# A graph-attention layer: turn-and-score in one matmul, division for two blocks at once, blocks of 125 targets in place of 121

## The chip, the cores and the metric

The kernel runs on one core of one Trainium2 chip. The metric is the device time of one execution in microseconds (us). Each time quoted is the median of several runs; a ratio is the mean time of one kernel's fast runs over the mean of the other's fast runs of the same rounds, so it is not quite the ratio of the medians. The engines are called PE (TensorE), DVE (VectorE), ACT (ScalarE), POOL (GpSimd) and SP (SyncE, which here only issues DMA). A one-hot is a matrix that has a 1 where an edge's node number matches the row and 0 elsewhere; PSUM is the memory that this kernel's matmuls write to; the span is the time from the first to the last instruction of the profiled run, and the quoted time is some 2 us more (317.16 against 314.9 before).

## The reference

There are 4096 nodes with 64 features, 50000 edges and 4 heads of 64 outputs. Cut to what matters:

```python
x_proj[h] = x @ weight[h]
score[h, e] = sum(x_proj[h, src] * att_src[h]) + sum(x_proj[h, dst] * att_dst[h])
score = where(score > 0, score, 0.2 * score)
output[h, dst] += exp(score[h, e]) * x_proj[h, src]        # over all edges
output[h, dst] /= (sum of exp(score[h]) over edges to dst) + 1e-8
```

## The kernel before

The first 120 us sort the edges on DVE into bins: one bin holds the edges whose target is in one block of `BD = 121` nodes and whose source is in one of 16 groups of 256 nodes. A bin has room for 128 edges, so a block is 16 tiles of 128 edges. Then 34 blocks are worked off. For each block:

```python
# load: the block's targets and sources, broadcast to all partitions (1 MB), DMA on SP
# onehot (DVE): oh[:,0] target one-hot, oh[:,1] and oh[:,2] source one-hots
# gather (PE, per tile t): three matmuls into xps[:, t, 0:72]
T.matmul(out=o, lhsT=oh[:, 1, e], rhs=xa[:, 2 * t, :], ...)            # 64 features + 8 scores
T.matmul(out=o, lhsT=oh[:, 2, e], rhs=xa[:, 2 * t + 1, :], ...)
T.matmul(out=o[:, Din:XC], lhsT=oh[:, 0, e], rhs=adb[:, b, :], ...)    # 8 target scores
# ACT: ex = exp(scores); xs = copy of the features
# turn (PE): 16 transposes of oh[:, 0], then two ACT copies to Sb
# weigh (DVE): wv = max(ex[:,0], ex[:,1]); val = xs * wv   (128 x 4096, bf16)
# scatter (PE): 16 denominators (4 columns), 32 accumulations of Sb[:, t, 0:BD]
# Finish: ACT copies the sums to aT (a second small copy adds 1e-8);
#         PE projects them with the weights; DVE: inv = 1/aT, res = pf * inv; DMA out
def run(self):
    self.onehot(0); self.gather(0); self.turn(0); self.onehot(1)
    for b in range(ND):
        self.load(b + 3)
        self.weigh(b, 2 if b == ND - 1 else 1)
        self.gather(b + 1)
        self.turn(b + 1)
        self.onehot(b + 2)
        if b:
            self.sink.give(b - 1)
        self.scatter(b)
    self.sink.give(ND - 1)
```

Each engine takes its own instructions in this program order, as PE's chain in the prediction shows: turn at 238.42, projection 239.33, denominators 239.82, sums 240.22, the next gather 241.97. `gather(b + 1)` and `turn(b + 1)` stand ahead of `scatter(b)`, so no matmul that feeds the next `val` waits behind one that needs this `val`.

## Time and profile before

| | before |
|---|---|
| time, median of the first 3 runs | 317.16 us |
| span of the profiled run | 314.9 us |
| to the start of the first `val` | 138.0 us |
| first to last `val` (33 intervals) | 162.6 us |
| from the start of the last `val` to the end | 14.3 us |
| busy in the stretch 147 to 200 us: PE, DVE, ACT | 100%, 96%, 73% |

The useful ruler is the start of `val`, DVE's big multiplication, once a block. The three parts add up to the span. The main views are in the prediction. Two more groups, by shape, are needed to see what the change takes out. The columns are line, engine, operation, tiles, shapes and count, then busy time and mean ns of one, then the idle time before it.

```profile
L437 ACT COPY Sb<-sp 128x1024 bf16<-128x1024 bf16 x68 | 66.3, 1039 | 0.0
L506 DVE TENSOR_TENSOR res<-pf,inv 121x256 f32<-121x256 f32 x34 | 14.4, 425 | 3.4 <-PE pf L501 0.4
```

The first is ACT's largest part, the copies of the turned one-hots. The second is the division, with 34 instructions.

### The profile page before, as it was taken

To read this page: it belongs to the slowest core of one execution; us is meant where nothing else is said; L and a number is where in the kernel's file an instruction comes from. 1 tells how busy PE (TensorE), PEld (TensorE's weight loads), DVE (VectorE), ACT (ScalarE), POOL (GpSimd) and SP (SyncE) were. 2 spreads that over 40 slices of the span, in tenths; PEclk is the share of its full clock that TensorE was granted. 3 is DMA by queue.
4 is the path that set the end of the run, shared out by engine and by line. 5 is a ranking of instruction groups with operands and counts; after the bars stand their busy time and mean duration, and the time that the engine had idled before them with its cause. 6 is when DMAs were issued, how large, how long until landed. Compare 5 with 4: busy or idle time off the path is not lost. (4 is left out here: it accounts for less than half of the span.)

```text
span 314.9 us, 9697 instructions
## 1 busy us (share of the span) xinstructions
PE 207.2 (66%) x4122; PEld 202.2 (64%) x4122; DVE 275.9 (88%) x552; ACT 172.9 (55%) x324; POOL 18.6 (6%) x40
## 2 busy tenths in 40 slices
PE   0049999000000000099999999999999999999970
PEld 0027999000000000099999999999999999999970
DVE  8999999993999995479999999999999999999960
ACT  3984000000999600067777768677686767768640
POOL 6800000002000005000000000000000000000000
PEclk9999555555555555579999999999999999999996
DMA  7200000002000002991865857667575766667110
GB/s 206 46 1 0 2 0 0 1 0 67 1 0 0 0 28 51 300 395 32 284 234 224 290 191 271 216 237 251 204 276 191 258 228 253 232 227 272 56 38 21
DMA packets 13551, 43.97 MB, mean 140 GB/s; under 512 B 3308, under 2 KB 8492, under 8 KB 9148
## 3 DMA queue, kind: packets, MB, share of 16 engines
q1 hardware_dynamic: 11332, 41.92, 37.7%
q10 hardware_dynamic: 1464, 0.70, 0.8%
q0 software_dynamic: 704, 0.66, 0.8%
q8 instruction: 34, 0.56, 0.8%
q14 instruction: 17, 0.14, 0.2%
HBM read 38.22 MB, written 5.05 MB: 137 GB/s over the span
## 5 line engine op out<-in xcount | busy, mean ns | idle before, releaser
L449 DVE TENSOR_TENSOR val<-xs,wv 128x4096 bf16<-128x4096 bf16 (+1 forms) x35 | 78.0, 2231 | 4.1 <-ACT xs L423 0.7
L437 ACT COPY Sb<-sp 128x1024 bf16<-128x1024 bf16 x68 | 66.3, 1039 | 0.0
L413 PE MATMUL xps<-xa,oh 128*128 128x72 bf16 x544 | 54.1, 194 | 14.5 <-DVE oh L401 14.5
L463 PE MATMUL acc<-Sb,val 128*128 128x121 bf16 x1088 | 63.6, 217 | 0.0
L413 PEld LDWEIGHTS <-oh 128*128 128x128 bf16 x544 | 50.4, 98 | 13.9 <-DVE oh L400 13.9
L463 PEld LDWEIGHTS <-val 128*128 128x128 bf16 x1088 | 58.5, 98 | 0.1
L415 PE MATMUL xps<-xa,oh 128*128 128x72 bf16 x544 | 53.7, 195 | 0.1
L417 PE MATMUL xps<-adb,oh 128*128 128x8 bf16 x544 | 52.8, 169 | 0.0
L415 PEld LDWEIGHTS <-oh 128*128 128x128 bf16 x544 | 49.4, 96 | 1.2 <-DVE oh L401 1.1
L417 PEld LDWEIGHTS <-oh 128*128 128x128 bf16 x544 | 50.1, 97 | 0.0
L400 DVE TENSOR_SCALAR oh<-bc,pF 128x4096 bf16<-128x4096 bf16 x34 | 43.5, 1281 | 4.6 <-DMA bc<-gat_bins 4.6
L420 ACT ACTIVATE ex<-xps 128x256 bf16<-128x256 f32 x34 | 13.4, 395 | 58.3 <-PE xps L417 58.3
L188 DVE TENSOR_TENSOR sA<-sB 128x256 f32<-128x256 f32 (+2 forms) x108 | 39.6, 408 | 1.8
L250 ACT ACTIVATE junk<-kr,nb 128x512 f32<-128x512 f32 x34 | 24.5, 722 | 25.6 <-DVE kr L301 24.5
L188 DVE TENSOR_TENSOR sB<-sA 128x256 f32<-128x256 f32 (+2 forms) x100 | 36.7, 408 | 1.7
L261 PE MATMUL cnt_ps<-sgn,sel 128*128 128x17 f32 (+1 forms) x6 | 1.7, 390 | 53.1 <-ACT sgn L253 53.1
L436 PE MATMUL sp<-identb,oh 128*128 128x128 bf16 x544 | 36.5, 221 | 0.0
L261 PEld LDWEIGHTS cnt_ps<-sgn,sel 128*128 128x128 f32 x6 | 1.4, 318 | 53.2 <-issue 53.2
L423 ACT CAST xs<-xps 128x1024 bf16<-128x1024 f32 x34 | 34.1, 1003 | 0.0
L436 PEld LDWEIGHTS <-oh 128*128 128x128 bf16 x544 | 31.4, 99 | 0.0
L401 DVE TENSOR_SCALAR oh<-bc,pF 128x2048 bf16<-128x2048 bf16 x34 | 25.4, 747 | 0.0
L345 PEld LDWEIGHTS at_ps<-uv,xT 64*128 64x128 f32 x132 | 25.1, 297 | 0.4 <-issue 0.4
(116 smaller groups left out, 255.7 us busy)
## 6 DMA issues: line engine op xcount, KB each, us to landing
bc<-gat_bins SPq DMA_DIRECT2D x34, 1024.0 KB
out_dram<-res SPq DMA_DIRECT2D x33, 121.0 KB
gat_sorted<-sA SPq DMA_DIRECT2D x2, 256.0 KB
eS<-in_edge_index_dram SPq DMA_DIRECT2D x1, 390.0 KB
eD<-in_edge_index_dram ACTq DMA_DIRECT2D x1, 390.0 KB
gat_bins<-tb ACTq DMA_DIRECT2D x9, 32.0 KB
out_dram<-res SPq DMA_DIRECT2D x1, 103.0 KB
win<-gat_sorted,wi POOLq DMA_INDIRECT x5, 2.6
```

What stands on the lines that cost most here:

```text
L188: V.tensor_tensor(out=av(d[:], o, [2 * h, n], [1, h]), in0=av(s[:], 0, [2 * h, n], [1, h]), in1=av(s[:], h, [2 * h, n], [1, h]), op=op)
L345: T.matmul(out=ps[:, b, :], lhsT=xT[:, b * step:b * step + P], rhs=uv[:, k, :], start=(b == 0), stop=True, skip_group_check=True)
L400: V.tensor_scalar(out=oh[:, 0:2, :], in0=bc[:], scalar1=pF[:, 0:1], scalar2=None, op0=OP.is_equal)
L401: V.tensor_scalar(out=oh[:, 2, :], in0=bc[:, 1, :], scalar1=pF[:, 1:2], scalar2=None, op0=OP.is_equal)
L413: T.matmul(out=o, lhsT=oh[:, 1, e], rhs=xa[:, 2 * t, :], start=(t % 4 == 0), stop=False, skip_group_check=True)
L415: T.matmul(out=o, lhsT=oh[:, 2, e], rhs=xa[:, 2 * t + 1, :], start=False, stop=False, skip_group_check=True)
L417: T.matmul(out=o[:, Din:XC], lhsT=oh[:, 0, e], rhs=adb[:, b, :], start=False, stop=True, skip_group_check=True)
L423: S.copy(out=xs[:], in_=xps[:, :, 0:Din])
L436: T.transpose(out=sp[:, i, :], in_=oh[:, 0, t * W2:(t + 1) * W2], identity=identb[:])
L437: S.copy(out=Sb[:, q * NT // 2:(q + 1) * NT // 2, :], in_=sp[:])
L449: V.tensor_tensor(out=av(val[:], h * Dout, [Dout, n], [C, NT], [1, Din]), in0=av(xs[:], 0, [0, n], [2, NT * Din // 2], [1, 2]), in1=av(wv[ ...
L463: T.matmul(out=acc[:, k * BD:(k + 1) * BD], lhsT=val[:, t, k * P:(k + 1) * P], rhs=Sb[:, t, 0:BD], start=False, stop=(t == NT - 1), skip_g ...
```

## The change

Its intent: one matmul with an identity beside the score columns does the turn and the target scores at once; epsilon enters as three bf16 terms through one-row matmuls, so that one copy of the sums suffices; reciprocal and division are done for two blocks at once; blocks of 125 targets make 33 blocks of 34; the first load is split over two queues. In place of one PSUM tile for all 16 gathers (128 numbers each a partition) there are two buffers of 6 (256 numbers each), so the gather is cut into three parts (6, 6 and 4 tiles), and these are put between the sums. The core of the diff, with cuts marked:

```diff
-BD = 121
+BD = 125
 ...
+    for i in range(3):                       # epsilon as three bf16 terms
+        V.tensor_copy(out=eps[:, i, :], in_=e0[:])
+        if i < 2:
+            V.tensor_copy(out=e1[:], in_=eps[:, i, :])
+            V.tensor_tensor(out=e0[:], in0=e0[:], in1=e1[:], op=OP.subtract)
 ...
-                T.matmul(out=o[:, Din:XC], lhsT=oh[:, 0, e], rhs=adb[:, b, :], start=False, stop=True,
+                T.matmul(out=ps[:, i, 0:S0], lhsT=oh[:, 0, e], rhs=adb[:, b, :], start=False, stop=True,
 ...
+            S.copy(out=xs[:, t0:t0 + n, 0:P + XC], in_=ps[:, 0:n, 0:P + XC])
 ...
-                self.gather(b + 1)
-                self.turn(b + 1)
+                self.gather(b + 1, 0)
                 self.onehot(b + 2)
                 if b:
-                    self.sink.give(b - 1)
-                self.scatter(b)
-            self.sink.give(ND - 1)
+                    self.sink.project(b - 1)
+                    if b % 2 == 0:
+                        self.sink.give(b - 2, 2)
+                self.sums(b, -1)
+                self.gather(b + 1, 1)
+                self.sums(b, 0)
+                self.gather(b + 1, 2)
+                self.sums(b, 1)
```

`sums(b, 0)` is the first matmul that needs `val` of block b; `sums(b, -1)` needs only wv.

More of the change, by code (lines that the diff above doesn't have):

```diff
@@ L110 @@
     pm8 = bits("pm8", 0, 7)
-    eps = cst.tile([P, 1], F32)
-    V.memset(eps[:], 1e-8)
+    e0 = cst.tile([1, H], F32)
+    e1 = cst.tile([1, H], F32)
+    eps = cst.tile([1, 3, H], BF16)
+    one = cst.tile([1, P], BF16)
+    nil = cst.tile([1, 3, H], BF16)
+    V.memset(e0[:], 1e-8)
+    V.memset(one[:], 1.0)
+    V.memset(nil[:], 0.0)
+    for i in range(3):
[3 more added lines that the diff above has]
+            V.tensor_tensor(out=e0[:], in0=e0[:], in1=e1[:], op=OP.subtract)
     goff = cst.tile([P, 1], F32)
@@ L150 @@
     xa = cst.tile([P, NB, XC], BF16)
-    adb = cst.tile([P, ND, 2 * H], BF16)
+    AB = P + 2 * H
+    adb = cst.tile([P, ND, AB], BF16)
     Wbd = cst.tile([P, 2, P], F32)
@@ L333, in tables @@
             S.copy(out=uv[:, :, 2 * i:2 * i + 2], in_=av(ps2[:], 0, [2, 2], [1, 2]))
-        S.copy(out=xa[:, :, 0:Din], in_=xf[:])
+        S.copy(out=xa[:, :, 2 * H:XC], in_=xf[:])
         xT = pr.tile([Din, ND * BD + P - BD], F32)
@@ L341, in tables @@
             S.copy(out=xT[:, 4 * q * P:4 * (q + 1) * P], in_=ps[:])
-        for k, (n, step, to) in enumerate(((NB, P, xa[:, :, Din:XC]), (ND, BD, adb[:]))):
+        for k, (n, step, to) in enumerate(((NB, P, xa[:, :, 0:2 * H]), (ND, BD, adb[:, :, P:AB]))):
             ps = pp1.tile([P, n, H], F32, name=f"at_ps{k}")
@@ L348, in tables @@
             S.mul(out=to[:, :, H:2 * H], in_=ps[:], mul=ALPHA)
+        S.copy(out=adb[:, :, 0:P], in_=av(identb[:], 0, [0, ND], [1, P]))
     NT = NR
@@ L374, in unpack @@
                               in_=self.tb[:, i, k, :])
+    CH = ((0, 6), (6, 6), (12, 4))
+    S0 = P + 2 * H
+    XW = 256
     class Blocks:
@@ L382, in __init__, with load, onehot @@
             self.bp = pool(name="blk", bufs=2)
-            self.psx = pool(name="ps_x", bufs=1, space=PSUM)
-            self.pss = pool(name="ps_s", bufs=2, space=PSUM)
+            self.psx = pool(name="ps_x", bufs=2, space=PSUM)
             self.psa = pool(name="ps_a", bufs=1, space=PSUM)
             self.sink = sink
-            self.bc, self.oh, self.xps, self.ex, self.xs, self.wv, self.Sb, self.val = ({} for _ in range(8))
-        def load(self, b):
+            self.bc, self.oh, self.ex, self.xs, self.wv, self.val = ({} for _ in range(6))
+        def load(self, b, engs=(nc.sync,)):
             if b < ND:
                 t = self.bcp.tile([P, 2, NT * W2], BF16, name="bc")
-                nc.sync.dma_start(out=t[:], in_=dataclasses.replace(bin_dram[b], ap=[[0, P], [NT * W2, 2],
-                                                                                    [1, NT * W2]]))
+                n = NT * W2 // len(engs)
+                for i, eng in enumerate(engs):
+                    eng.dma_start(out=t[:, :, i * n:(i + 1) * n],
+                                  in_=dataclasses.replace(bin_dram[b, 0, i * NT // len(engs)],
+                                                          ap=[[0, P], [NT * W2, 2], [1, n]]))
                 self.bc[b] = t
-        def onehot(self, b):
+        def onehot(self, b, parts=1):
             if b < ND:
@@ L399, in onehot, with gather @@
                 oh = self.bp.tile([P, 3, NT * W2], BF16, name="oh")
-                V.tensor_scalar(out=oh[:, 0:2, :], in0=bc[:], scalar1=pF[:, 0:1], scalar2=None, op0=OP.is_equal)
-                V.tensor_scalar(out=oh[:, 2, :], in0=bc[:, 1, :], scalar1=pF[:, 1:2], scalar2=None, op0=OP.is_equal)
+                n = NT * W2 // parts
+                for i in range(0, NT * W2, n):
+                    V.tensor_scalar(out=oh[:, 0:2, i:i + n], in0=bc[:, :, i:i + n], scalar1=pF[:, 0:1], scalar2=None,
+                                    op0=OP.is_equal)
+                    V.tensor_scalar(out=oh[:, 2, i:i + n], in0=bc[:, 1, i:i + n], scalar1=pF[:, 1:2], scalar2=None,
+                                    op0=OP.is_equal)
                 self.oh[b] = oh
-        def gather(self, b):
+        def gather(self, b, c):
             if b >= ND:
@@ L408, in gather @@
             oh = self.oh[b]
-            xps = self.psx.tile([P, NT, P], F32, name="xps")
-            for t in range(NT):
-                o = xps[:, t, 0:XC]
+            if c == 0:
+                self.ex[b] = self.bp.tile([P, 2, H, NT, 2], BF16, name="ex")
+                self.xs[b] = self.bp.tile([P, NT, XW], BF16, name="xs")
+            ex, xs = self.ex[b], self.xs[b]
+            t0, n = CH[c]
+            ps = self.psx.tile([P, CH[0][1], XW], F32, name="ps")
+            for i in range(n):
+                t = t0 + i
@@ L412, in gather @@
                 e = slice(t * W2, (t + 1) * W2)
-                T.matmul(out=o, lhsT=oh[:, 1, e], rhs=xa[:, 2 * t, :], start=(t % 4 == 0), stop=False,
+                T.matmul(out=ps[:, i, P:P + XC], lhsT=oh[:, 1, e], rhs=xa[:, 2 * t, :], start=(i % 2 == 0), stop=False,
                          skip_group_check=True)
-                T.matmul(out=o, lhsT=oh[:, 2, e], rhs=xa[:, 2 * t + 1, :], start=False, stop=False,
+                T.matmul(out=ps[:, i, P:P + XC], lhsT=oh[:, 2, e], rhs=xa[:, 2 * t + 1, :], start=False, stop=False,
@@ L416, in gather @@
                          skip_group_check=True)
-                T.matmul(out=o[:, Din:XC], lhsT=oh[:, 0, e], rhs=adb[:, b, :], start=False, stop=True,
+                T.matmul(out=ps[:, i, 0:S0], lhsT=oh[:, 0, e], rhs=adb[:, b, :], start=False, stop=True,
                          skip_group_check=True)
-            ex = self.bp.tile([P, 2, H, NT, 2], BF16, name="ex")
-            S.activation(out=av(ex[:], 0, [2, NT], [2 * NT, 2 * H], [1, 2]),
-                         in_=av(xps[:], Din, [P, NT], [1, 2 * H], [0, 2]), func=ACTF.Exp)
@@ L422, in gather @@
-            xs = self.bp.tile([P, NT, Din], BF16, name="xs")
-            S.copy(out=xs[:], in_=xps[:, :, 0:Din])
-            self.ex[b], self.xs[b] = ex, xs
-        def turn(self, b):
-            if b >= ND:
-                return
-            oh = self.oh.pop(b)
-            Sb = self.bp.tile([P, NT, W2], BF16, name="Sb")
-            for q in range(2):
-                sp = self.pss.tile([P, NT // 2, W2], BF16, name="sp")
-                for i in range(NT // 2):
-                    t = q * NT // 2 + i
-                    T.transpose(out=sp[:, i, :], in_=oh[:, 0, t * W2:(t + 1) * W2], identity=identb[:])
-                S.copy(out=Sb[:, q * NT // 2:(q + 1) * NT // 2, :], in_=sp[:])
-            self.Sb[b] = Sb
+            S.activation(out=av(ex[:], 2 * t0, [2, n], [2 * NT, 2 * H], [1, 2]),
+                         in_=av(ps[:], P, [XW, n], [1, 2 * H], [0, 2]), func=ACTF.Exp)
@@ L440, in weigh @@
+            S.copy(out=xs[:, t0:t0 + n, 0:P + XC], in_=ps[:, 0:n, 0:P + XC])
+            if c == len(CH) - 1:
+                self.oh.pop(b)
         def weigh(self, b, parts=1):
-            xs, ex = self.xs.pop(b), self.ex.pop(b)
+            xs, ex = self.xs[b], self.ex.pop(b)
             wv = self.bp.tile([P, H, NT, 2], BF16, name="wv")
@@ L449, in weigh @@
                 V.tensor_tensor(out=av(val[:], h * Dout, [Dout, n], [C, NT], [1, Din]),
-                                in0=av(xs[:], 0, [0, n], [2, NT * Din // 2], [1, 2]),
+                                in0=av(xs[:], S0, [0, n], [XW, NT], [1, Din]),
                                 in1=av(wv[:], h * 2 * NT, [2, n * NT], [0, Din // 2], [1, 2]), op=OP.mult)
             self.val[b] = val
-        def scatter(self, b):
-            val, wv, Sb = self.val.pop(b), self.wv.pop(b), self.Sb.pop(b)
-            acc = self.psa.tile([P, AW], F32, name="acc")
-            for t in range(NT):
-                T.matmul(out=acc[:, 2 * BD:AW], lhsT=Sb[:, t, :], rhs=av(wv[:], 2 * t, [2 * NT, H]), start=(t == 0),
-                         stop=(t == NT - 1), skip_group_check=True)
-            for k in range(2):
-                for t in range(NT):
-                    T.matmul(out=acc[:, k * BD:(k + 1) * BD], lhsT=val[:, t, k * P:(k + 1) * P], rhs=Sb[:, t, 0:BD],
-                             start=False, stop=(t == NT - 1), skip_group_check=True)
-            self.sink.take(b, acc[:])
@@ L467, in run, with sums @@
-        def run(self):
-            self.onehot(0)
-            self.gather(0)
-            self.turn(0)
+        def sums(self, b, k):
+            xs = self.xs[b]
+            if k < 0:
+                self.acc = self.psa.tile([P, AW], F32, name="acc")
+                wv = self.wv.pop(b)
+                for i in range(3):
+                    T.matmul(out=self.acc[:, 2 * BD:AW], lhsT=one[:], rhs=self.sink.first[:, i, :], start=(i == 0),
+                             stop=False, skip_group_check=True)
+                for t in range(NT):
+                    T.matmul(out=self.acc[:, 2 * BD:AW], lhsT=xs[:, t, 0:P],
+                             rhs=av(wv[:], 2 * t, [2 * NT, H]), start=False, stop=(t == NT - 1), skip_group_check=True)
+                return
+            val = self.val[b]
+            for t in range(NT):
+                T.matmul(out=self.acc[:, k * BD:(k + 1) * BD], lhsT=val[:, t, k * P:(k + 1) * P],
+                         rhs=xs[:, t, 0:BD], start=False, stop=(t == NT - 1), skip_group_check=True)
+            if k == 1:
+                self.val.pop(b), self.xs.pop(b)
+                self.sink.take(b, self.acc[:])
@@ L471, in run @@
+        def run(self, parts=1):
+            self.onehot(0, parts)
+            for c in range(len(CH)):
+                self.gather(0, c)
             self.onehot(1)
@@ L483 @@
+                self.gather(b + 1, 1)
+                self.sums(b, 0)
+                self.gather(b + 1, 2)
+                self.sums(b, 1)
+            self.sink.project(ND - 1)
+            n = 2 - ND % 2
+            self.sink.give(ND - n, n)
     class Finish:
         def __init__(self, ctx):
+            self.first = eps
             self.fp = ctx.enter_context(tc.tile_pool(name="fin", bufs=2))
             self.psf = ctx.enter_context(tc.tile_pool(name="ps_f", bufs=1, space=PSUM))
-            self.aT = {}
@@ L491, in take @@
         def take(self, b, acc):
-            aT = self.fp.tile([P, AW], F32, name="aT")
-            S.copy(out=aT[:, 0:2 * BD], in_=acc[:, 0:2 * BD])
-            S.activation(out=aT[:, 2 * BD:AW], in_=acc[:, 2 * BD:AW], func=ACTF.Identity, bias=eps[:, 0:1])
-            self.aT[b] = aT
-        def give(self, b):
-            aT = self.aT.pop(b)
-            pf = self.psf.tile([P, C], F32, name="pf")
-            for k in range(2):
-                T.matmul(out=pf[0:BD, k * P:(k + 1) * P], lhsT=aT[:, k * BD:(k + 1) * BD], rhs=Wbd[:, k, :],
-                         start=(k == 0), stop=True, skip_group_check=True)
-            inv = self.fp.tile([P, H], F32, name="inv")
-            V.reciprocal(out=inv[:], in_=aT[:, 2 * BD:AW])
-            res = self.fp.tile([P, H, Dout], F32, name="res")
-            V.tensor_tensor(out=res[0:BD], in0=av(pf[0:BD], 0, [Dout, H], [1, Dout]),
-                            in1=av(inv[0:BD], 0, [1, H], [0, Dout]), op=OP.mult)
-            n = min(BD, N - b * BD)
-            nc.sync.dma_start(out=out[b * BD:b * BD + n, :], in_=res[0:n].rearrange("p h o -> p (h o)"))
+            if b % 2 == 0:
+                self.aT = self.fp.tile([P, 2, AW], F32, name="aT")
+                self.pf = self.psf.tile([P, 2, C], F32, name="pf")
@@ new lines, in take, with project, give @@
+            S.copy(out=self.aT[:, b % 2, :], in_=acc)
+        def project(self, b):
+            for k in range(2):
+                T.matmul(out=self.pf[0:BD, b % 2, k * P:(k + 1) * P], lhsT=self.aT[:, b % 2, k * BD:(k + 1) * BD],
+                         rhs=Wbd[:, k, :], start=(b % 2 == 0 and k == 0), stop=True, skip_group_check=True)
+        def give(self, b, n):
+            inv = self.fp.tile([P, 2, H], F32, name="inv")
+            V.reciprocal(out=inv[0:BD, 0:n], in_=self.aT[0:BD, 0:n, 2 * BD:AW])
+            res = self.fp.tile([P, 2, H, Dout], F32, name="res")
+            V.tensor_tensor(out=res[0:BD, 0:n], in0=av(self.pf[0:BD], 0, [Dout, n * H], [1, Dout]),
+                            in1=av(inv[0:BD], 0, [1, n * H], [0, Dout]), op=OP.mult)
+            for i in range(n):
+                m = min(BD, N - (b + i) * BD)
+                nc.sync.dma_start(out=out[(b + i) * BD:(b + i) * BD + m, :],
+                                  in_=res[0:m, i].rearrange("p h o -> p (h o)"))
@@ L511 @@
     class Total:
         def __init__(self, total):
+            self.first = nil
             self.total = total
@@ L518, in take, with project, give @@
             V.tensor_tensor(out=self.total[:, b, :], in0=acc, in1=self.total[:, b, :], op=OP.add)
-        def give(self, b):
+        def project(self, b):
+            pass
+        def give(self, b, n):
             pass
@@ L565 @@
         for b in range(3):
-            blocks.load(b)
+            blocks.load(b, (nc.sync, nc.scalar) if b == 0 else (nc.sync,))
         for i in range(1, NI):
             win.unpack(i, nc.scalar, nc.scalar)
-        blocks.run()
+        blocks.run(2)
     order.close()
@@ L592 @@
             with ExitStack() as st:
+                V.tensor_scalar(out=total[:, :, 2 * BD:AW], in0=total[:, :, 2 * BD:AW], scalar1=1e-8, scalar2=None,
+                                op0=OP.add)
                 fin = Finish(st)
@@ L595 @@
                     fin.take(b, total[:, b, :])
-                    fin.give(b)
+                    fin.project(b)
+                    if b % 2 or b == ND - 1:
+                        fin.give(b - b % 2, b % 2 + 1)
 _INS = ['x', 'edge_index', 'weight', 'att_src', 'att_dst']
```

## The prediction

> **What bounds the kernel now.** I first read the rows of slices: the run has a sort of about 120 us on VectorE (DVE) and, from about 132 us on, 34 blocks of 121 target nodes each, in which TensorE (PE) and DVE both show nines. The change touches the blocks and a few constants at the start, so I then asked for the busy time of stretches within the blocks:
>
> ```profile
> core 0: us, PE busy (x) PEld busy (x) DVE busy (x) ACT busy (x) POOL busy (x), PEclk, DMA share, GB/s
> 147.00:200.00 53.00, 53.00 (x1250) 52.87 (x1248) 50.94 (x64) 38.71 (x66) 0.00 (x0) 1.00 0.66 237
> 250.00:300.00 50.00, 50.00 (x1170) 49.66 (x1167) 47.97 (x62) 36.60 (x61) 0.00 (x0) 1.00 0.61 214
> ```
>
> PE is always busy, at full clock (1.00); DVE at 96%, the rest being handover between its instructions; ScalarE (ACT) at 73%. DMA is at two thirds. So PE and DVE are both close to the limit. The chain that ended last blames PE alone:
>
> ```profile
> PE 25%; ACT 0%; DVE 0%; issue 0%
> PE acc L463 9%; PE sp L436 4%; PE xps L413 4%; PE pf L501 3%; PE xps L415 3%; PE acc L459 2%; PE xps L417 0%; ACT aT L493 0%; DVE res L506 0%; DVE inv L504 0%
> ```
>
> The DVE timeline of one block shows that this is half the story:
>
> ```profile
> 154.61 1.28 DVE L400 TENSOR_SCALAR oh<-bc,pF 128x4096 bf16<-128x4096 bf16 x1
> 155.81 0.75 DVE L401 TENSOR_SCALAR oh<-bc,pF 128x2048 bf16<-128x2048 bf16 x1
> 156.47 0.17 DVE L504 RECIPROCAL inv<-aT 128x4 f32<-128x4 f32 x1
> 156.73 0.42 DVE L506 TENSOR_TENSOR res<-pf,inv 121x256 f32<-121x256 f32 x1
> 157.07 0.21 DVE L444 TENSOR_TENSOR wv<-ex 128x128 bf16<-128x128 bf16 x1
> 157.39 2.29 DVE L449 TENSOR_TENSOR val<-xs,wv 128x4096 bf16<-128x4096 bf16 x1
> 159.60 1.28 DVE L400 TENSOR_SCALAR oh<-bc,pF 128x4096 bf16<-128x4096 bf16 x1
> ```
>
> No line carries an idle time, and the start-to-start times are 1.20, 0.66, 0.26, 0.34, 0.32 and 2.21, together **4.99 us a block**. On PE the chain of one block reads, in order of time:
>
> ```profile
> core 0 of [0], span 314.9 us
> ...
> 238.42 0.91 PE sp L436 x16
> 239.33 0.49 PE pf L501 x4
> 239.82 0.40 PE acc L459 x16
> 240.22 1.73 PE acc L463 x32
> 241.97 0.07 PE xps L415
> ```
>
> From 241.97 to the next transposes at 243.41 is the gather, 1.44 us, so PE needs 0.91 + 0.49 + 0.40 + 1.73 + 1.44 = 4.97. Both engines fill a block of 4.99. To gain, a change must shorten both, without putting a wait between them.
>
> [...]16 transposes of 128 columns take 0.91 us (57 ns each), 16 denominators of 4 columns 0.40 us (25 ns). [...]the half-size `val` of the last block took 1222 ns. [...]The trace has 361 ns at 242 and 1003 ns at 1024 elements, so 0.82.
>
> **The change part by part.** Is the fast path kept? I counted the drawn edges: the fullest bin of 125 targets by 256 sources holds 123, under the 128 of a window. So the slow loop is not entered, and 33 blocks take the place of 34.
>
> *PE a block.* The 16 transposes go (-0.91). The third gather matmul widens from 8 to 136 columns: about 24 ns becomes 60, 16 times, +0.58. Accumulation widens from 121 to 125: +0.05. Three one-row matmuls bring in epsilon: +0.08. Sum: 4.97 - 0.91 + 0.58 + 0.05 + 0.08 = 4.77.
>
> *ACT a block.* Two copies of Sb (start to start 0.91 each) and one aT instruction go. In their place the copies carry 200 instead of 64 columns a tile: 1200, 1200 and 800 elements, by the slope above 1.15, 1.15 and 0.82 us, with three exponentials before them that add 0.14 to 0.17 each. With overlap about 3.6 us against 3.5: not a bound.
>
> *DVE a block.* `val` and the one-hots keep their size[...]. Reciprocal and division come once for two blocks: 512 elements, [...]0.27 + 0.61 = 0.88 for two instead of 1.20. Mean: 4.99 - 0.60 + 0.44 = 4.83.
>
> If engines were all, a block would take 4.83, and 33 blocks some 10 us less than 34. **The new wait is what I believe instead.** PE's order is now: gather part 0 of the next block, projection, denominators, gather part 1, first half of the sums (needs `val`), gather part 2, second half. So gather part 2 of block b+1 stands behind a matmul that waits for `val` of block b, and `val` of b+1 needs gather part 2 of b+1. From the end of one `val` to the end of the next there are, in order: 0.10 to the first matmul (the first weight load comes 0.05 after its producer in two waits of this trace, the matmul next); 0.89 for the first half of the sums, 16 x 55.6 ns; 0.51 for gather part 2, four tiles of (33.5 + 33.5 + 60) ns; 0.20 from the start of the last matmul's record to ACT (a record of 0.17 to 0.22, then 0.03, less the slot counted already); 0.14 for the exponential and 0.82 for the copy of 800 elements; 0.03 from ACT to DVE (137.98 to 138.01) and 2.29 for `val`.
>
> Sum **4.98**. In the time from one `val` to the next DVE also has the one-hots (1.86) and wv (0.32), which fit beside this; but in every second block it has the paired 0.88 as well, and then DVE alone needs 2.21 + 1.86 + 0.88 + 0.32 = **5.27**. In the other blocks it needs 4.39, but the loop holds it to 4.98. The pairing thus makes uneven work, and the loop stops the light block from giving back what the heavy one took. 15 intervals at 5.27 and 17 at 4.98 are 163.7 us from the first `val` to the last. Before, that was 138.01 to 300.61, 162.6 us. The block saved is eaten.
>
> *Start.* The three-term epsilon adds seven tiny DVE operations that wait for each other (such steps start 0.19 apart in this trace: 1.01, 1.20, 1.39) and some memsets: 6 x 0.19 + 0.07 + 0.2 = +1.4 us. The first edge instruction starts at 5.32, with the constants done at 5.40 and the edges landed at 5.30, so all of this is on the path:
>
> ```profile
> 5.24 0.16 DVE L544 MEMSET sB<- 128x121 f32 x1
> 5.30 1.28 ACT L250 ACT_TABLE_LOAD   x1 [5.30 <-DMA eS<-in_edge_index_dram]
> 5.32 0.39 DVE L548 TENSOR_SCALAR sli<-eS 128x391 int32<-128x391 int32 x1
> ```
>
> The identity copy into the table (4224 elements, about 3.6 us on ACT) falls where ACT waits 24.5 us for DVE: free. The first load split over two queues and the first one-hots in two parts let PE start about 1 us sooner, but the gather, at half clock there, is longer by about as much: -0.2 to the first `val`.
>
> *End.* The last `val` to the end of its sums was 4.49 us (300.61 to 305.10), with backlog on PE. After, PE has less before it: about 3.3, so -1.2. The projection, division and the last store stay.
>
> Sum: 314.9 + 1.4 - 0.2 + 1.1 - 1.2 = 316.0 us of span, and 2.2 more for the time (317.14 against 314.9): **318 us**.
>
> **The rivals.** *Engines alone*: the loop is slacker than I think or DVE hides it, blocks take 4.83, the whole some 308 us. For it: both busiest engines lose work, and a change like this is made to gain. Against it: the 5.27 of the heavy block is plain DVE work, and the order on PE is fixed. *Loop longer*: 0.2 us more in each handover[...] lifts only the 17 light intervals: 321 to 322. [...]*PE bound*: if the widened gather costs 80 ns rather than 60 a tile, PE needs 5.1: again 320.
>
> **Range and chances.** 32 intervals times 0.1 us of error on the loop is about 3 us each way, and start and end may err by 1.5. From 312 to 323 covers that; the time is most likely within 2% (310.8 to 323.5).
>
> **What would show it.** Right: starts of `val` alternately about 4.98 and 5.27 apart; DVE idle before wv or `val` waiting for ACT in light blocks; PE idle before the first half of the sums waiting for `val`; the first edge instruction near 6.7 us. Wrong: even spacing at 4.83 without idle time on DVE; `val` far from 2.29 us; ACT packed.

At the marks, rules that no trace of this case shows are cut, and one rival that rested on them (that `val` gets slower by the new row stride; it took 2292 ns in both kernels). No term of a sum is cut: PE's 4.77, DVE's 4.83 and 5.27, the loop's 4.98 and the total of 318 us can be added up as they stand. Two terms had such a rule behind them and now rest on what the traces show, and a third was an estimate that failed:

- 0.27 + 0.61 for the paired reciprocal and division: the 0.61 came from a rule. Measured after: 0.29 + 0.60 from start to start (216.71, 217.00 and 217.60 in the timeline below), 692 ns for a division of 512 elements.
- 60 ns for 136 columns: the 57 ns of 128 columns, scaled, give 60.6 (an estimate). Measured from start to start between 147 and 300 us: 61 ns after (median), and 27 ns for the 8 columns before, so that the widening is 16 x 34 ns = 0.54 and not 0.58.
- 0.08 for the three one-row matmuls: three times the 25 ns of a denominator. Measured: 0.16 (e6_both, below).

That `val` and the one-hots keep their time was an assumption; it held (2292, 1283 and 747 ns after; 2292, 1281 and 747 before). That a matmul waits its turn behind one that waits for `val`, on which the new wait rests, was not tested by the profile before; e1_order tests it (light blocks fall from 4.91 to 4.42 with gather part 2 put ahead). The half clock at the first gather is 0.50, from 132 to 136 us of the profile before.

## The result, and the profile after

The changed kernel takes **320.68 us** (320.63 to 320.94, 4 runs) against 316.99 before; the ratio is 1.011, with a 95% interval of 1.009 to 1.014. It counts as the same at 2%, and is a little slower. In the ruler's parts:

| part | before | predicted | after |
|---|---|---|---|
| to the first `val` | 138.0 | 139.2 | 139.9 |
| first to last `val` | 162.6 | 163.7 | 167.8 |
| last `val` to the end | 14.3 | 13.1 | 11.2 |
| span | 314.9 | 316.0 | 318.9 |

The same windows as before show both busy engines with gaps now. The columns are the stretch, its length, then busy time and count on PE, PE's weight loads, DVE, ACT and POOL, then PE clock, DMA share and GB/s.

```profile
147.00:200.00 53.00, 51.37 (x1053) 48.92 (x1050) 48.57 (x52) 39.52 (x72) 0.00 (x0) 1.00 0.56 197
250.00:300.00 50.00, 48.05 (x975) 45.36 (x976) 45.10 (x46) 35.98 (x67) 0.00 (x0) 1.00 0.63 217
```

PE fell from 100% to 96 or 97%, DVE from 96% to 90 or 92%; the PE clock is full as before (1.00), and DMA is on the whole not busier (0.56 and 0.63, before 0.66 and 0.61). No engine is full, so waits decide. The list of waits says who waits for whom (total, times, longest; lines picked from it):

```profile
DVE val L464 <- ACT xs L451: 8.8, 18, 0.5
PEld L484 <- DVE val L464: 8.1, 16, 1.0
DVE oh L422 <- DMA bc<-gat_bins: 6.1, 9, 2.9
PE acc L484 <- DVE val L464: 5.7, 16, 0.8
DVE oh L422 <- PE ps L447: 1.3, 5, 0.3
```

The first two, with the fourth, are the loop that the prediction named: `val` waits for the copy on ACT, and the sums wait for `val`. The third was not in the prediction: the one-hots wait for their load. Of its 6.1 us, 3.6 are two waits at the start, before the first `val`; seven lie in heavy blocks. (The last one is probably the same wait: the matmuls named had ended over 2 us before, for the one-hots of 225.36 at 221.8, and five of the heavy blocks show it where others show the load.) On DVE's timeline, two blocks with their waits in brackets:

```profile
212.34 2.29 DVE L464 TENSOR_TENSOR val<-xs,wv 128x4096 bf16<-128x4096 bf16 x1 [0.49 <-ACT xs L451]
214.84 1.29 DVE L422 TENSOR_SCALAR oh<-bc,pF 128x4096 bf16<-128x4096 bf16 x1 [0.21 <-DMA bc<-gat_bins]
216.04 0.75 DVE L424 TENSOR_SCALAR oh<-bc,pF 128x2048 bf16<-128x2048 bf16 x1
216.71 0.20 DVE L534 RECIPROCAL inv<-aT 125x8 f32<-125x8 f32 x1
217.00 0.69 DVE L536 TENSOR_TENSOR res<-pf,inv 125x512 f32<-125x512 f32 x1
217.60 0.21 DVE L459 TENSOR_TENSOR wv<-ex 128x128 bf16<-128x128 bf16 x1
217.92 2.29 DVE L464 TENSOR_TENSOR val<-xs,wv 128x4096 bf16<-128x4096 bf16 x1
220.13 1.28 DVE L422 TENSOR_SCALAR oh<-bc,pF 128x4096 bf16<-128x4096 bf16 x1
221.33 0.75 DVE L424 TENSOR_SCALAR oh<-bc,pF 128x2048 bf16<-128x2048 bf16 x1
222.12 0.23 DVE L459 TENSOR_TENSOR wv<-ex 128x128 bf16<-128x128 bf16 x1
222.83 2.29 DVE L464 TENSOR_TENSOR val<-xs,wv 128x4096 bf16<-128x4096 bf16 x1 [0.49 <-ACT xs L451]
```

The reader sees a heavy block (212.34 to 217.92, 5.58 us, with the paired division) and a light one (217.92 to 222.83, 4.91). The light one ends in 0.49 us of waiting for ACT. This goes on through the run: 17 intervals of 4.91 and 15 heavy ones that average 5.62, from 5.29 to 6.15. SP's queue in the same stretch:

```profile
207.22 0.68 SPq L540 DMA_DIRECT2D out_dram<-res  x2
207.94 0.83 SPq L411 DMA_DIRECT2D bc<-gat_bins  x2
217.71 0.68 SPq L540 DMA_DIRECT2D out_dram<-res  x2
218.43 0.82 SPq L411 DMA_DIRECT2D bc<-gat_bins  x2
```

Two stores and two loads go out together, once a pair. The first of the loads issued at 207.94 is what the one-hots wait for until 214.84, 6.9 us later. This closes a second loop over a pair of blocks: load to one-hots 6.90, one-hots 1.87 (214.84 to 216.71), reciprocal 0.29, division 0.71 until the stores go out at 217.71, and 0.72 until the next loads at 218.43. The sum is 10.49 us, and the loads are 10.49 apart.

The PE-and-ACT loop can be read off the end of the chain of work that ended last (start, length, what), for the last light interval:

```profile
302.84 2.31 DVE val L464
305.14 0.05 issue
305.19 1.05 PE acc L484 x16
306.25 0.03 PE ps L443
...
306.78 0.23 ACT ex L449
307.00 0.71 ACT xs L451
```

`val` ends at 305.14, the first half of the sums starts 0.05 later, the exponential starts at 306.78, and the copy that starts at 307.00 ends just before the last `val` at 307.75: 4.91 us from `val` to `val`. The prediction had 4.98.

### The profile page after: what moved, and what is told of

The parts are those of the page before. It is cut to its first block, busy times and chain, and to the rows that moved or that the text cites. A ratio compares the mean times of both kernels' runs of the same rounds, so it can differ in the third digit from the quotient of the medians.

```text
span 318.9 us, 8497 instructions
## 1 busy us (share of the span) xinstructions
PE 205.2 (64%) x3575; PEld 192.3 (60%) x3575; DVE 272.0 (85%) x525; ACT 178.7 (56%) x350; POOL 18.7 (6%) x40
## 5 line engine op out<-in xcount | busy, mean ns | idle before, releaser
L451 ACT CAST xs<-ps 128x1200 bf16<-128x1200 f32 (+1 forms) x99 | 103.2, 1042 | 0.0
L443 PE MATMUL ps<-xa,oh 128*128 128x72 bf16 x528 | 73.9, 197 | 14.4 <-DVE oh L424 13.7
L447 PE MATMUL ps<-adb,oh 128*128 128x136 bf16 x528 | 76.6, 226 | 0.0
L445 PE MATMUL ps<-xa,oh 128*128 128x72 bf16 x528 | 73.9, 198 | 0.4 <-DVE oh L424 0.3
L484 PE MATMUL acc<-xs,val 128*128 128x125 bf16 x1056 | 68.8, 218 | 5.7 <-DVE val L464 5.7
L449 ACT ACTIVATE ex<-ps 128x96 bf16<-128x96 f32 (+1 forms) x99 | 24.4, 246 | 73.1 <-PE ps L447 43.0
L443 PEld LDWEIGHTS <-oh 128*128 128x128 bf16 x528 | 52.3, 99 | 12.6 <-DVE oh L422 12.6
L445 PEld LDWEIGHTS <-oh 128*128 128x128 bf16 x528 | 52.1, 99 | 3.0 <-DVE oh L424 2.0
L447 PEld LDWEIGHTS <-oh 128*128 128x128 bf16 x528 | 52.1, 99 | 0.0
L422 DVE TENSOR_SCALAR oh<-bc,pF 128x4096 bf16<-128x4096 bf16 (+1 forms) x34 | 42.5, 1251 | 7.5 <-DMA bc<-gat_bins 6.1
L358 PE MATMUL at_ps<-uv,xT 64*128 64x4 f32 x130 | 25.2, 331 | 0.0
L424 DVE TENSOR_SCALAR oh<-bc,pF 128x2048 bf16<-128x2048 bf16 (+1 forms) x34 | 24.9, 731 | 0.0
L529 PE MATMUL pf<-Wbd,aT 128*125 128x128 f32 x132 | 21.8, 288 | 1.3 <-ACT aT L525 0.9
```

The source lines that it names most:

```text
L358: T.matmul(out=ps[:, b, :], lhsT=xT[:, b * step:b * step + P], rhs=uv[:, k, :], start=(b == 0), stop=True, skip_group_check=True)
L422: V.tensor_scalar(out=oh[:, 0:2, i:i + n], in0=bc[:, :, i:i + n], scalar1=pF[:, 0:1], scalar2=None, op0=OP.is_equal)
L424: V.tensor_scalar(out=oh[:, 2, i:i + n], in0=bc[:, 1, i:i + n], scalar1=pF[:, 1:2], scalar2=None, op0=OP.is_equal)
L443: T.matmul(out=ps[:, i, P:P + XC], lhsT=oh[:, 1, e], rhs=xa[:, 2 * t, :], start=(i % 2 == 0), stop=False, skip_group_check=True)
L445: T.matmul(out=ps[:, i, P:P + XC], lhsT=oh[:, 2, e], rhs=xa[:, 2 * t + 1, :], start=False, stop=False, skip_group_check=True)
L447: T.matmul(out=ps[:, i, 0:S0], lhsT=oh[:, 0, e], rhs=adb[:, b, :], start=False, stop=True, skip_group_check=True)
```

## The experiments

Twelve kernels ran, each in 3 rounds beside the kernel before and with a profile, and all gave correct results. Times are medians; the ruler's parts and mean intervals come from each profile. The first load lands at a time that varies: in five kernels with the same start (the changed one, e1, e2, e7, e12) the first one-hots start between 132.5 and 134.1, so a first `val` later or earlier by 1.6 us says little about an edit.

| run | time | first `val` | first to last | rest | light / heavy |
|---|---|---|---|---|---|
| before | 317.0 | 138.0 | 162.6 | 14.3 | 4.99, but for three (4.39, 5.42, 3.13) |
| after | 320.7 | 139.9 | 167.8 | 11.2 | 4.91 / 5.62 |
| e1_order | 321.7 | 141.0 | 167.5 | 11.2 | 4.42 / 6.20 once settled |
| e2_unpaired | 313.9 | 140.9 | 160.6 | 10.8 | 4.99, but for three |
| e3_ahead | 319.0 | 140.9 | 164.0 | 12.8 | 4.91 / 5.28, one of 6.57 |
| e4_before125 | 311.5 | 138.0 | 159.3 | 12.3 | 4.99, the last 5.01 |
| e5_eps | 321.8 | 138.8 | 169.7 | 11.3 | 4.91 / 5.75 |
| e6_both | 311.5 | 141.0 | 156.6 | 12.3 | 4.54 / 5.28 |
| e7_stores | 319.8 | 140.7 | 162.7 | 15.0 | 4.91 / 5.28 |
| e8_all | 311.3 | 140.6 | 156.9 | 12.4 | 4.51 / 5.33 once settled |
| e9_both_act | 307.1 | 139.7 | 154.0 | 11.4 | 4.42 / 5.28 |
| e10_best | 307.2 | 139.9 | 154.0 | 11.4 | 4.42 / 5.29 |
| e11_act | 319.3 | 139.3 | 166.7 | 11.2 | 4.91 / 5.55 |
| e12_bd121 | 323.8 | 141.0 | 168.0 | 14.1 | 4.88 / 5.29, one of 6.14 |

### e1_order: the loop through PE and ACT taken away

```diff
-                self.sums(b, 0)
                 self.gather(b + 1, 2)
+                self.sums(b, 0)
```

> The changed kernel, with gather part 2 of the next block put ahead of the first half of the sums on PE; nothing else moves. Theory (a loop val -> first half of sums -> gather part 2 -> copy on ACT -> next val holds the light blocks at 4.91 us): the waits of val for the ACT copy (8.8 us in the changed kernel) go, light and heavy blocks even out near DVE's own mean of 4.83, the first to last val takes 155 to 160 us in place of 167.8, and the time is 308 to 313 us; the late loads may stay. Rival (heavy blocks and late loads alone set the time, light blocks only wait because something else is full): light blocks stay near 4.9, time within 1 us of 320.7.

Measured: 321.71 us, so the theory's time was missed by 9 us. But neither theory saw what came. The light blocks did fall, from 4.91 to 4.42, DVE's own work, so the loop was real; the rival's light blocks near 4.9 did not appear. The heavy ones grew by as much:

```profile
202.34 2.29 DVE L464 TENSOR_TENSOR val<-xs,wv 128x4096 bf16<-128x4096 bf16 x1
205.68 1.29 DVE L422 TENSOR_SCALAR oh<-bc,pF 128x4096 bf16<-128x4096 bf16 x1 [1.04 <-DMA bc<-gat_bins]
```

Where the changed kernel waited 0.21 us at this place, this one waits 1.04. A pair takes 10.62 us (4.42 + 6.20, from the fifth interval on), against 10.56 in the changed kernel over the same intervals. Something else held the pair, and the time won in the light block was waited away in the heavy one. The kernel is not shown to be slower than the changed one: the runs overlap (320.11 to 322.15, against 320.63 to 320.94), and in the profile it is the first `val` that comes 1.1 us later, while the intervals take 0.3 us less.

### e2_unpaired: the pairing taken away

Reciprocal, division, tile and store for each block by itself; the other parts stay. Cut to its core:

```diff
                     self.sink.project(b - 1)
-                    if b % 2 == 0:
-                        self.sink.give(b - 2, 2)
+                    self.sink.give(b - 1, 1)
```

> The changed kernel with reciprocal, division and store for each block by itself, as before, PE order kept. Theory (the pairing makes heavy blocks of 5.27 us on DVE, which the loop does not let light blocks give back): all blocks take DVE's 4.99, a little above the loop's 4.91; 32 intervals are 159.7 us and the time 312 to 314, although DVE has MORE work (about 0.16 us a block, 5 us in all). The one-hots should also wait less for loads, as stores no longer go out two by two ahead of them. Rival (less DVE work is worth what it saves): slower than the changed kernel by up to 5 us, 321 to 326.

Measured: 313.94 us, ratio to before 0.990 (0.987 to 0.992). All intervals were 4.99 or 5.00 but three: one with a late load (6.08), and the first and last, at 4.91. So about 0.16 us a block of extra work on DVE made the kernel 6.7 us faster. This edit removes the heavy blocks and also spreads the stores and loads, so by itself it doesn't say which of the two paid.

### e3_ahead: the loads issued earlier

```diff
-            self.bcp = pool(name="bc", bufs=3)
+            self.bcp = pool(name="bc", bufs=4)
 ...
-                self.load(b + 3)
+                self.load(b + 4)
```

(and four loads in place of three before the first block)

> The changed kernel with a fourth bc buffer and each load issued one block earlier. Theory (heavy blocks of the changed kernel average 5.62 where DVE's work is 5.29, because two loads and two stores are issued together behind the paired division and come late): heavy blocks fall to 5.29, light ones stay at 4.91, 17 x 4.91 + 15 x 5.29 = 162.8 in place of 167.8, time about 315.7. Rival (the loads are late for want of bandwidth): no change, 320 to 321.

Measured: 318.96 us. Heavy blocks fell to 5.28 and light ones stayed at 4.91, as the theory said, so the rival (bandwidth) falls. The total of the intervals is 164.0 and not 162.8, because one interval at the start was 6.57 (its wv waited 0.80 for ACT); the first `val` came 0.9 us later and the rest was 1.6 us longer, so of the 3.9 us won in the intervals only 1.7 showed, and the 315.7 was missed.

### e4_before125: the block size alone

```diff
-BD = 121
+BD = 125
```

in the kernel before, nothing else.

> The kernel before with blocks of 125 in place of 121 targets, nothing else. One block of 4.99 us less: 33 blocks, time 317.0 - 5.0 = 312; PE has 32 accumulations of 125 columns in place of 121, 0.05 us a block, so PE may bind at 5.02 and the time be up to 313. Rival (wider accumulation [...]costs more on PE): no gain, 316 or more.

Measured: **311.47 us**, ratio 0.983 (0.980 to 0.985). One line of the change, by itself, gains 5.6 us, as expected, but not all of it by the block saved. From the first `val` to the end of the last division it takes 165.7 us in place of 168.7, so 3.0 less. That is near the difference of PE's work as the prediction counts it (34 x 4.97 less 33 x 5.02, 3.3): PE binds here, as the expectation feared, for the last intervals are 5.01 and DVE waits up to 1.97 us for a projection. The other 2.4 us come after the last division, 5.8 in place of 8.2. Blocks of 125 leave a last block of 96 targets and blocks of 121 one of 103. By the trace's packet records the store of 96 rows takes from 304.50 to 305.75, up to 16 packets at a time, and that of 103 rows from 307.44 to 312.73, one or two at a time. The rest of the change costs 320.7 - 311.5 = 9.2 us.

### e6_both: both loops taken away

The edits of e1_order and e3_ahead together.

> The changed kernel with both edits that did little alone: gather part 2 ahead of the first half of the sums, and a fourth bc buffer with loads one block earlier. After the first four runs the theory is that two loops of nearly the same length hold a pair of blocks: the one through PE and ACT (10.2 us a pair, seen alone when loads are early) and one through the loads (two stores and two loads are issued only after the paired division; the first load is needed 6.9 us later: 10.6 us a pair, seen alone when PE's order is changed). With both gone DVE's own work is left, 4.40 + 5.28 = 9.68 a pair: 16 pairs are 154.9 us from first to last val in place of 167.8, time about 308. Rival (the edits' gains don't add, PE at 4.8 a block or bandwidth binds): 315 or more.

Measured: 311.47 us, ratio 0.982 (0.979 to 0.985). One edit alone gained nothing (1.0 us slower, within the noise), the other 1.7 us, and both together 9.2 us. The time missed its 308, however: a pair took 9.82 us and not 9.68. The window says why:

```profile
200.00:250.00 50.00, 50.00 (x1046) 48.43 (x1043) 47.74 (x51) 38.86 (x72) 0.00 (x0) 1.00 0.68 247
```

PE is busy without a gap, so its own work is 4.91 us a block. This is 0.14 more than the 4.77 that the prediction added up, and by chance the same number as the PE-and-ACT loop. One mis-sized term is the three one-row matmuls, which start at 210.39 in this trace, with the denominators next at 210.55: 0.16 us where the prediction had 0.08.

### e7_stores: the stores from another queue

```diff
-                nc.sync.dma_start(out=out[(b + i) * BD:(b + i) * BD + m, :],
-                                  in_=res[0:m, i].rearrange("p h o -> p (h o)"))
+                nc.gpsimd.dma_start(out=out[(b + i) * BD:(b + i) * BD + m, :],
+                                    in_=res[0:m, i].rearrange("p h o -> p (h o)"))
```

> The changed kernel with three bc buffers and the old PE order, only the two output stores issued from GpSimd's queue, so that loads no longer stand behind them on SyncE's. Theory (loads are late because of their place in the queue): heavy blocks 5.29, light ones 4.91 as with four buffers, and without the four loads crowding the start: time 315.5 to 317.5. Rival (a third buffer is too few whatever the queue, or bandwidth): heavy blocks stay at 5.6, time 320 to 321.

Measured: 319.83 us. With three buffers and SP's loads no longer behind the stores, heavy blocks are 5.28 and none waits for a load, so it was the stores ahead of them that made them late. (The edit changes two things, the place in the queue and the engine that issues, and e12_bd121 will show that the place alone is not enough.) The intervals take 162.7 us, 5.1 less. The time was missed all the same: the stretch from the last `val` to the end grew from 11.2 to 15.0 us, with the last store issued from POOL at 308.80 in a span of 318.4. A store from POOL ends this kernel later than one from SP (here the span ended 9.9 us after the end of the last division at 308.50, in the changed kernel 6.1 us after the one at 312.84).

### e5_eps, e8_all: the epsilon terms on POOL

The block that makes the epsilon terms is moved behind POOL's other constants, with `G.` in place of `V.`; e8_all adds it to e6_both.

> The changed kernel with the epsilon terms, the row of ones and the zeros made on GpSimd after its other constants, not on VectorE at the start. In the changed kernel the first edge instruction starts at 7.16 us where it started at 5.32 before. Theory (these ten operations lie on the path in full): first edge instruction back at about 5.3, time shorter by 1.8 us, 318.9. Rival (VectorE waits for the edges anyway, or the delay is absorbed by the later wait for the windows): 320.7 within 0.5.

> All three edits at once: PE order, fourth buffer, epsilon on GpSimd. If the parts add: the time of e6_both less that of the epsilon alone, about 308 - 1.8 = 306, faster than the kernel before by 3.4%. If one of the loops is not gone, 313 or more.

Measured: 321.81 and 311.31 us; both expectations were missed. The first comparison of the sort starts at 7.83 instead of 9.09, so 1.26 us of the start is won and not 1.8: the edges themselves now come last, and the first edge instruction waits 0.29 us for them. In e5_eps the first `val` is 1.1 us earlier, but the heavy blocks average 5.75 and the intervals take 1.9 us more. In e8_all the first `val` is only 0.4 us earlier than in e6_both. In both, two intervals show the division waiting 0.44 or 0.45 us, which e6_both does not have. Why the loads of e5_eps came later than those of the changed kernel with the same block code is not settled.

### e9_both_act, e10_best, e11_act: the epsilon back on ACT

```diff
-                for i in range(3):
-                    T.matmul(out=self.acc[:, 2 * BD:AW], lhsT=one[:], rhs=self.sink.first[:, i, :], start=(i == 0),
-                             stop=False, skip_group_check=True)
 ...
-            S.copy(out=self.aT[:, b % 2, :], in_=acc)
+            S.copy(out=self.aT[:, b % 2, 0:2 * BD], in_=acc[:, 0:2 * BD])
+            S.activation(out=self.aT[:, b % 2, 2 * BD:AW], in_=acc[:, 2 * BD:AW], func=ACTF.Identity,
+                         bias=eps[:, 0:1])
```

e9_both_act is this on top of e6_both; e10_best also issues the fourth load only with the first block; e11_act is this on the changed kernel alone.

> e6_both, with epsilon added by ScalarE in the copy of the sums, as in the kernel before, in place of three one-row matmuls and ten VectorE operations at the start. In e6_both PE is busy without a gap and a pair takes 9.82 us, not DVE's 9.68. Theory (PE's own work of 4.91 a block is the bound left; the three matmuls are 0.16 of it): the pair falls to DVE's 9.68 to 9.70, light blocks from 4.54 to 4.42, first to last val from 156.6 to 155; the first key comparison starts about 1.3 us sooner than 9.10; time 308.5 to 310. Rival (the copy on ACT now decides, as it gets longer by 0.2 us a block): pair stays 9.8 or grows, 311 or more.

> e9_both_act, with three loads before the first block as in both kernels, the fourth issued with the first block's. Theory (four loads at once delay the first one: first one-hots at 133.5 to 134.1 in the runs with four, 131.8 to 132.5 with three): first one-hots near 131.9, time 1 to 1.5 us below e9_both_act, about 307.5 to 308.5, 3% under the kernel before. Rival (the spread of the first load is chance): as e9_both_act within 0.5.

> The changed kernel with epsilon on ScalarE as before, PE order and three buffers as changed. e5_eps started the sort 1.3 us sooner and yet ended 1.1 us later, as heavy blocks waited longer for loads. Theory (the gain at the start is real but the pair is held by the loads, whose time varies): first key comparison at 7.8, first val near 138.8, pairs still 10.4 to 10.7, time 319 to 321.5. Rival (GpSimd's part in e5_eps cost something in the blocks): 319.0 to 319.5, with heavy blocks at 5.6 as in the changed kernel.

Measured: e9_both_act takes **307.13 us**, ratio to before 0.971 (0.966 to 0.976), and e10_best 307.21 us, ratio 0.969 (0.964 to 0.974). Both beat both kernels by over 2%. The first is even below its 308.5 to 310, as the time after the last `val` fell too, from 12.3 to 11.4. In e9_both_act the pair is 4.42 + 5.28 = 9.70, DVE's own work, and PE has gaps again:

```profile
200.00:250.00 50.00, 49.47 (x1031) 48.39 (x1029) 48.30 (x53) 41.30 (x83) 0.00 (x0) 1.00 0.69 244
```

So PE's work was the bound in e6_both, and the three tiny matmuls a block were the difference: 49.47 of 50 us is about 4.80 a block. ACT takes the second copy at 82 or 83% busy. The rival of e10_best was right: with three loads the first one-hots start at 133.04, with four at 132.76, so the spread of that first load (131.8 to 134.1 over these runs) is not made by the fourth one. The record could have said so before: e1_order, e2_unpaired and e7_stores, with three loads, had started at 133.6 to 134.1. e11_act took 319.30 us, and the pairs stay at 10.46, held by the loads. That fits its theory, but its rival (POOL's part in e5_eps cost something) also: heavy blocks are 5.55, nearer to the changed kernel's 5.62 than to the 5.75 of e5_eps. This run doesn't separate the two.

### e12_bd121: the changed kernel with blocks of 121

```diff
-BD = 125
+BD = 121
```

> The changed kernel with blocks of 121 as before, so 34 blocks. Theory (one block more costs half a pair): +5.2 us, time 326, that is 3% slower than the kernel before; all of the rest of the change is then a loss of about 9 us, as the kernel before with blocks of 125 (311.5) said. Rival (narrower sums give PE 0.05 us a block and shorten the loop): 324.

Measured: 323.82 us, ratio to before 1.020 (1.016 to 1.024). The extra block costs only 3.1 us, less than the theory's 5.2. The time is the rival's 324, but its reason gives only about 0.5 us (light blocks of 4.88 in place of 4.91). What counts is that heavy blocks are 5.29 and only one of them has a late load:

```profile
213.97 1.28 DVE L422 TENSOR_SCALAR oh<-bc,pF 128x4096 bf16<-128x4096 bf16 x1
```

The loads before were issued at 207.44 and the one-hots of 213.97 did not wait, so the first came within 6.53 us, where the changed kernel's took 6.90. The order of stores and loads is the same; what differs is that a store has 121 rows and not 125. The trace doesn't name the engine of a packet, but it has busy shares and packet times. Here is the busy share of the 16 DMA engines, in slices of 0.25 us and tenths, from 0.94 us before the two loads are issued; the changed kernel (207 to 217) first, e12_bd121 (206.5 to 216.5) second:

```profile
DMA  0000332689999999999898999998643333352000
DMA  0000667798099997999979998989953010300000
```

The stores come first in each. With 125 rows they keep 0.3 of the engines busy, with 121 rows 0.6 to 0.7, and by the packet records their 250 and 242 packets take from 208.00 to 211.95, mostly five at a time, and from 207.46 to 208.79, about eleven at a time. And after 125 rows the loads end with a tail in which 0.3 of the engines work on alone, beyond 215.5. So it looks as if a few engines (5 of 16 are 0.31), longer busy with stores, finish their part of the loads late; without engine names this is inferred and not shown, and why the number of rows should matter is not shown either. No run changed the rows of the stores alone, but this one changes little else inside a pair of blocks.

## Why the prediction was right or wrong

The time, 318 predicted and 320.7 measured, lay in the range. By its own steps:

- **The bound before**, DVE and PE both at 4.99 us: right for both. In e4_before125 DVE's blocks are 4.99 and, where PE binds at the end, 5.01, the prediction's 4.97 and 0.05.
- **The engine sums after.** DVE: predicted 5.27 and 4.39, measured 5.28 and 4.42 once nothing else binds (e9_both_act). ACT: predicted some 3.6 us, 72 to 75% busy in the windows, no bound. PE: predicted 4.77, measured 4.91 (e6_both), a mis-sized term of which the one-row matmuls are 0.08.
- **The loop**, predicted 4.98, measured 4.91 in every light block, with the waits that the prediction named. e1_order and e6_both show it is a cause: with the third gather part ahead of the sums, light blocks fall to 4.42 and 4.54.
- **The pairing makes uneven work that the loop doesn't give back.** Shown in e3_ahead and e7_stores, where light and heavy are 4.91 and 5.28.
- **The step that failed is "In the time from one `val` to the next DVE also has ..."**, which took the one-hots as ready when DVE comes to them. In the changed kernel they wait for their load in most heavy blocks, which average 5.62 where the prediction had 5.27. The pairing also pairs the stores, and the next two loads stand behind these on SP, which makes the load loop of 10.5 us a pair. The block size has a part in it: with stores of 121 rows heavy blocks but one are 5.29 (e12_bd121). The loop that the prediction found allows 10.19 a pair (4.91 + 5.28), so it was only the second-longest. Taking it away alone won nothing (e1_order); taking away the load loop alone won what the prediction would have had (5.62 to 5.28 in heavy blocks).
- **The start**, predicted +1.4 for the epsilon terms: the first edge instruction starts at 7.16 (predicted near 6.7, before 5.32), the first comparison at 9.09 instead of 7.55, so +1.54. The steps that wait for each other came 0.19 to 0.33 apart, not 0.19. The split first load and the one-hots in two parts didn't give the 0.2: from the first one-hots to the first `val` it takes 7.4 us, and 6.9 or more in every kernel with the change, against 6.2 in the two without it. The first `val` is 139.9 where the prediction had 139.2.
- **The end**, predicted 1.2 us shorter: the sums end 3.49 us after the last `val` (before 4.49), so 1.0. Another 2.1 us came from the stretch after the last division, 6.1 us in place of 8.2, which was not predicted: it goes with the block size, as in e4_before125, where the last store has 96 rows and not 103. (It is not alone there: over the eleven kernels with blocks of 125 and stores on SP the stretch is 5.7 to 7.7.) It hid part of the loss, and so did the time outside the span, 1.8 us where the prediction had 2.2. That the total came within 3 us is in part luck: without these two it would have been some 323, at the edge of the range.

Of the rivals, "engines alone" (308) is what e9_both_act and e10_best reach, once both loops and the three matmuls are gone. The longer loop did not occur: light blocks were 4.91. "PE bound" was not the bound of the changed kernel, but it waited just behind it, at the 4.91 of e6_both.

Where the expected gain went: blocks of 125 are worth 5.6 us by themselves, some 3 for the block and 2.4 for the last store (e4_before125); 1.9 us went into the later first `val`; and the rest, with the work taken from PE and DVE, went into the two loops of nearly the same length, either of which was enough to hold it.

## What to carry to other kernels

Before work is moved or merged in a software pipeline, write down for each big instruction what must pass between one instance and the next on all engines, queues included, because a loop longer than the busiest engine's work decides however much work is taken away. Merging small work of two iterations makes iterations uneven and bunches the transfers that follow it; a loop of one iteration cannot use the light one to make up for the heavy one. And if taking away one wait wins nothing, look for a second of about the same length before giving up the theory: here the edits alone gained nothing and 1.7 us, together 9.2. And look at the number of rows of a store: here mostly five packets ran at once with 125 rows and about eleven with 121, up to 16 with 96 and one or two with 103, and with that went when the next loads came and when the kernel ended.

## Costs that these traces show

- Stores ahead of a load: two stores of 125 rows took 3.95 us and the first of two 1 MB loads behind them 6.90 us to its first use (the changed kernel); with 121 rows it was 1.33 us and at most 6.53 (e12_bd121). One store of 103 rows took 5.29 us (the kernel before), one of 96 rows 1.25 (e4_before125).
- From one engine's end to the start of another that waits, in the changed kernel: 0.03 us from ACT to DVE (`xs` to `val`), 0.05 us from DVE to a weight load on PE (`val` to the sums), and 0.02 to 0.04 us from the modelled end of a matmul to ACT.
- The 16 denominators take 0.40 us in the kernel before, 25 ns each, but a group of three matmuls with one row of weights took 0.16 us in place of three times 25 ns (210.39 to 210.55 in e6_both).
